# A two-layer Hawk and HGRN2 step: the fourth gate block in three passes, the gates by Silu, and a last stage in four spans

## The chip, the cores and the metric

The kernel runs on one core of a Trainium2 chip. Its time is the device time of one launch in microseconds (us). TensorE (PE in the profile, with PEld for its weight loads), VectorE (DVE), ScalarE (ACT), GpSimd (POOL) and SyncE (SP, which here only starts transfers) each run their own instruction stream and wait for one another by semaphores. Three runs of the kernel before gave 1030.36, 1031.57 and 1032.78 us, so the median is 1031.57 us.

## The reference

Two layers work on 1056 tokens: one prompt of 1024 and 8 short sequences of 4. Each layer normalises its input, multiplies it by one wide matrix, mixes along time, gates, multiplies by an output matrix and adds the input. Cut to what matters here:

```
u = rmsnorm(x) @ w_in;  xb, gate = u[:1536], u[1536:]
xc = causal_conv4(xb)
r  = sigmoid(xc_block @ w_r + b_r)      # 16 blocks of 96 channels
ig = sigmoid(xc_block @ w_i + b_i)
a  = exp(-8 * softplus(-lam) * r)
h  = scan(a, sqrt(1 - a*a) * (ig * xc))
x1 = x + (h * silu(gate)) @ w_out       # end of the first layer
q, f, v, g = split(rmsnorm(x1) @ b_w_in)
...                                     # HGRN2: chunked recurrence with a matrix state, 8 heads
x2 = x1 + (rmsnorm(o) * silu(g)) @ b_w_out
y  = rmsnorm(x2) * final_gain           # the last stage
```

The model is 1024 wide and the recurrence 1536. Everything is float32.

## The kernel before

**Layout.** Tokens lie along the free axis, channels along the partitions. In the first layer the 1056 columns are worked in three chunks of 352 (CH). The wide products are not made in plain float32: each operand is split into a high part in the float32r type and a remainder, also float32r, and mm3 (L262 to L264) adds three matmuls into one PSUM tile: high by high, high by low, low by high. So "a product over k" is three instructions, with two weight tiles. Weights come from HBM as float32 and are split by ACT (L403) and by POOL or DVE (L346).

**The first layer.** The 1536 channels are four groups (g) of 384, each in three tiles (j) of 128 partitions. For a group the program makes the product, the convolution (L521, L524), the split of the result into X (L529 for the high part), the gate products and the recurrence (lru). A gate block has 96 channels, a tile 128. So a group has four blocks on three tiles: three blocks lie whole on one tile each, the fourth has 32 rows on each of the three. The first three blocks take three passes each from X. For the fourth, three transfers per chunk collect the float32 rows into the tile ST (36 transfers in all), and one plain float32 matmul (L592) multiplies them with the weights gs; its result td goes by Tanh (L594) and three more transfers into R. The recurrence then uses Exp (L601, L603) and Sqrt (L611) on ACT. The output gate silu(z) is made from Tanh: ACT writes tanh(z/2) (L546, L553, L556), DVE adds 1 and multiplies by z (L557 and its two sisters), and a factor 0.5 goes into the product with h (L638).

**Order.** A class Flow holds every operation with its engine, a cost in us, what it reads and writes, and a priority; it plans all engines against each other, forward and backward, then searches, and emits each engine's list in the planned order. The wide products are main operations, whose order on PE is the program's; small products on PE (gates, norm sums, spreads) are not, and the planner puts them between main ones, held back by a slack `side` (1.2 us in the first layer). For ACT the planner charges 1.29 us when the function set changes and holds that Tanh, Exp and Silu are one set and Sqrt another.

**Norms.** The sum of squares over channels is a matmul of the squares with a column of ones (norm_sum, L299), which leaves one number per token on the partition axis. ACT takes the root, DVE the reciprocal. To spread the factor over the partitions, DVE multiplies it into the identity (a diagonal tile dg, L473 and L476 in the first layer, L1728 and L1732 at the end), and one float32 matmul of ones with dg (L478, L1738) gives the factor of each token on all partitions.

**Start.** While the first data arrives PE gets 36 float32 products of ones with ones (WARM, L753), lowest in priority, so that the planner may use them as filling.

**Last stage.** The output product of the second layer is made over column spans (OUT): 512, 288 and 256. In each span eight tiles (m) of 9 matmuls are added to x1 by DVE (L1781) and squared by ACT (L1783), and POOL adds up the squares (L1792). The sums of a span, as a main operation, come before product 3 of the next (RM), the spread before product 6 (SM); then finish multiplies eight tiles by the factor and by the gain: three with ACT (L1755) and POOL (L1756) after ACT has copied the factor out of PSUM (L1751), five on DVE (L1758), and sends each to HBM (L332), alternately from SP's and ACT's queue. In the last span the last squares go straight into the sum on PE, and two products (L1796) fill PE until the spread.

Of the kernel before, what the change touches and what calls it, by code (L numbers as in the profile page):

```python
# [14 lines left out]
F32 = mybir.dt.float32  # L15
# [4 lines left out]
ALU = mybir.AluOpType  # L20
PSUM = bass.MemoryType.PSUM
KB = 5
WARM = 36
# [11 lines left out]
RM, SM = 3, 6  # L35
OUT = ((0, 512), (512, 288), (800, 256))
# [194 lines left out]
def tile_trunk(ctx: ExitStack, tc: tile.TileContext, xT, prm, hc, w0, wg, wo0, w1, wo1, s_in,  # L231
# [41 lines left out]
    ones = const.tile([128, 128], F32, name="ones")  # L273
# [22 lines left out]
    def norm_sum(sums, acc, n, start, stop):  # L296

        for s, (a, u) in zip(sums, spans(n)):
            T.matmul(s[:u], acc[:, a:a + u], ones[:, :1], start=start, stop=stop)  # L299
# [18 lines left out]
    with ExitStack() as l0:  # L318
# [39 lines left out]
        gs = fixed("gs", [96, 2, 96])  # L358
# [10 lines left out]
        xos = ring("xo", NXO)  # L369
# [7 lines left out]
        ST = C("ST")  # L377
        rows = [C("sg") for _ in range(6)]
# [81 lines left out]
        def norm(acc, own=None, sums=None, sumk=()):  # L460
# [3 lines left out]
            dg, dk = own or next(xbs)  # L464
# [4 lines left out]
            for i, (s, (_, u)) in enumerate(zip(sums, spans(CH))):  # L469
# [17 lines left out]
        def conv(g, head=False):  # L487

            items = []
            for j in range(3):  # L490
# [3 lines left out]
                def evac(c, ps, pk, by=None, j=j, m=m, mine=mine):  # L494
# [31 lines left out]
                    w = slice(32 * j, 32 * j + 32)  # L526
                    dma(ST[w, chunk(c)], t[w], (tk,), (("ST", j, c),), 1, 45)
# [9 lines left out]
        def gate(g, js=range(3), late=False):  # L537

            items = []
            for j in js:  # L540

                def evac(c, ps, pk, by=None, j=j):
                    sg, sk = sgs[g][j, c] = halves[g % 2][3 * j + c]
                    if late:
                        t, tk = next(ts)
                        act(CH, lambda: S.activation(t, ps[:, :CH], AF.Tanh, scale=0.5), (pk,), (tk,), 0)  # L546
                        dve(CH, lambda: V.scalar_tensor_tensor(t, t, 1.0, ps[:, :CH], op0=ALU.add, op1=ALU.mult), (pk, tk), (tk,), 0)
                        dve(CH, lambda: V.scalar_tensor_tensor(sg, sg, 0.5, t, op0=ALU.mult, op1=ALU.mult), (tk, sk), (sk,), 1, True)
                        return
                    if by:  # L550
                        t, tk = next(ts)
                        dve(CH, lambda: V.tensor_tensor(sg, ps[:, :CH], by[0], op=ALU.mult), (pk, by[1]), (sk,), 0)
                        act(CH, lambda: S.activation(t, sg, AF.Tanh, scale=0.5), (sk,), (tk,), 0)  # L553
                        dve(CH, lambda: V.scalar_tensor_tensor(sg, t, 1.0, sg, op0=ALU.add, op1=ALU.mult), (tk, sk), (sk,), 1, True)
                        return
                    act(CH, lambda: S.activation(sg, ps[:, :CH], AF.Tanh, scale=0.5), (pk,), (sk,), 0)  # L556
                    dve(CH, lambda: V.scalar_tensor_tensor(sg, sg, 1.0, ps[:, :CH], op0=ALU.add, op1=ALU.mult), (pk, sk), (sk,), 0)  # L557
# [4 lines left out]
        def lru(g):  # L562
# [9 lines left out]
            dma(gs.rearrange("p a b -> p (a b)"), wg[g][:96, 768:], (), (("gs",),), 2, 74)  # L572
            prev = [(0.0, None)] * 3
            for c in range(NCH):
# [3 lines left out]
                ta, ti = R[:, 0], R[:, 1]  # L578
                tak, tik = ([("R", s, i, j) for j in range(3)] for i in range(2))
                for i, hb in ((0, hbr), (1, hbi)):  # L580
                    for j in range(3):
# [10 lines left out]
                    fl.add("PE", 0.62, lambda ps=ps, i=i, c=c: T.matmul(ps[:96, :CH], gs[:, i, :], ST[:96, chunk(c)], start=True, stop=True),  # L592
                           (("gs",), *(("ST", j, c) for j in range(3))), (pk,), 0)
# [21 lines left out]
                for j in range(3):  # L615
# [22 lines left out]
                    dve(CH, lambda h=h, sg=sg: V.scalar_tensor_tensor(sg, h, 0.5, sg, op0=ALU.mult, op1=ALU.mult), (hk, sk), (sk,), 3, True)  # L638
# [34 lines left out]
        def out_last(src):  # L673
# [42 lines left out]
            for c in range(NCH):  # L716
# [11 lines left out]
                for m, x, xk in rows:  # L728
                    scaled_parts(c, m, x, xk, bc, bk, pc("g1", m), ("P",), G if m % 4 == 3 else V, 4)
                    dma(xnd[m][:, chunk(c)], x, (xk,), (("xnd", m, c),), 5)  # L730

        def first1(i, c):
# [8 lines left out]
            else:  # L741
                t, tk = next(ts)
                act(CH, lambda: S.activation(t, ps[:, :CH], AF.Tanh, scale=0.5), (pk,), (tk,), 0)
                for o, a, b, ks in ((ST, lc, lbc, [("ST", j, c) for j in range(3)]), (a_rows[0], lcn, lc, [("a", 0, c)])):
# [5 lines left out]

        warm, wk = next(hg)
        for _ in range(WARM):
            fl.add("PE", 0.25, lambda: T.matmul(warm[:, :128], ones, ones, start=True, stop=True), (), (wk,), 9)  # L753
# [121 lines left out]
        rest += [(ST[:, :512], *(("ST", j, c) for j in range(3) for c in range(2)))]  # L875
        raw1 = [(), rest[:1], rest[1:3], rest[3:5], (), ()]

        def begin(c, first, last):
# [18 lines left out]
            bc, bk = norm(accs[c], next(xrs))  # L897
# [54 lines left out]
    with ExitStack() as l1:  # L952
# [760 lines left out]
        accs, sqs, dgs, sb = cycle(spare[:2]), cycle(spare[2:5]), cycle(spare[5:7]), spare[7]  # L1713
        nr2 = cycle([(fixed(f"nr2{i}", [128, 4], F32, p1), ("nr2", i)) for i in range(2)])

        def roots(n, sums, ready):

            r, rk = next(nr2)
            dg, dk = next(dgs)
            f, u = n // 128, n % 128  # L1720
# [7 lines left out]
            dve(128 * f, lambda: V.tensor_tensor(dg[:, :128 * f].rearrange("p (i n) -> p i n", i=f),  # L1728
                                                 ident[:, None, :].to_broadcast([128, f, 128]),
                                                 r[:, :f, None].to_broadcast([128, f, 128]), op=ALU.mult), (rk,), (dk,), 0)  # L1730
            if u:
# [138 lines left out]
```

## Time and profile before

| view | figure |
|---|---|
| profiled execution, its time | 1031.86 us |
| its span (first to last instruction) | 1030.1 us |
| median of three runs | 1031.57 us |
| PE busy | 1021.1 us, 99% |
| DVE busy | 810.8 us, 79% |
| ACT busy | 578.1 us, 56% |
| POOL busy | 496.5 us, 48% |
| ACT table loads | 34, mean 1.283 us |
| granted TensorE clock | 0.997 |
| start of the last stage's products | 981.12 us |
| last product pass issued, sums begin | 1019.1 to 1019.23 us |

A row of the timeline reads: start in us, duration in us, engine, line, operation, output<-input, size, and in brackets the idle time ahead of it with what ended that. Matmuls overlap in the array, so a matmul's duration is longer than the distance to the next one. What a matmul costs PE is the distance from start to start. Plain float32 matmuls leave two records each (the fourth block's row with "x2" is one instruction), float32r ones leave one.

### The profile page before, as it was taken

The page shows a single profiled execution, that of the slowest core. Times are in us where ns is not written, and L with a number is a line of the kernel's source. Part 1 is how long each engine was busy: PE and PEld are TensorE (multiplying, and loading weights), DVE is VectorE, ACT ScalarE, POOL GpSimd, SP SyncE. Part 2 cuts the span into 40 slices and gives each one's busy share as a digit, 9 for nine tenths or more (in the row PEclk, how much of TensorE's full clock was granted, in tenths as well). Part 3 has the DMA queues.
Part 4 walks back from the last instruction along what each step waited for, and adds up shares of the span by engine and source line. Part 5 has one row for each costly group of instructions (what it writes and reads, how often), then busy time and mean ns, then how long its engine had stood idle before and what let it go on. Part 6 is the DMA issues. An engine that isn't in the chain of part 4 may idle for free.

```text
span 1030.1 us, 26451 instructions
## 1 busy us (share of the span) xinstructions
PE 1021.1 (99%) x10118; PEld 996.4 (97%) x10118; DVE 810.8 (79%) x1641; ACT 578.1 (56%) x1322; POOL 496.5 (48%) x569
## 2 busy tenths in 40 slices
PE   9999999999999999999999999999999999999997
PEld 9999999999999999999999999999999999999986
DVE  7999785867888699436599999798989799986436
ACT  8788747876775785335454463626363636552334
POOL 0117353544526236636425656555555557533544
PEclk9999999999999999999999999999999999999998
DMA  9201112112852487426474244343535353687204
GB/s 299 78 17 56 57 48 74 52 54 76 257 178 59 133 270 223 160 83 219 136 213 138 73 147 132 130 148 111 167 111 168 102 159 122 207 246 209 87 1 169
DMA packets 107854, 138.30 MB, mean 134 GB/s; under 512 B 23632, under 2 KB 85072, under 8 KB 107728
## 3 DMA queue, kind: packets, MB, share of 16 engines
q1 hardware_dynamic: 105424, 133.85, 42.1%
q10 hardware_dynamic: 2304, 2.77, 0.8%
q8 instruction: 79, 1.29, 0.5%
q14 instruction: 47, 0.39, 0.1%
HBM read 89.99 MB, written 41.61 MB: 128 GB/s over the span
## 4 chain that ended last, share of the span: by engine, by line
PE 93%; DVE 2%; DMA 2%; ACT 1%; issue 1%; POOL 1%; SPq 0%; POOLq 0%; DVEq 0%; ACTq 0%
PE mm L262 27%; PE mm L264 26%; PE mm L263 26%; PE hg L1085 2%; PE hg L592 1%; PE hg L262 1%; PE hg L264 1%; PE hg L263 1%; PE hg L753 1%; PE hg L1232 1%; PE hg L1287 1%; PE hg L1289 1%; DMA k<-yd 1%; PE mm L1085 0%; DMA vt<-sg 0%
## 5 line engine op out<-in xcount | busy, mean ns | idle before, releaser
L262 PE MATMUL mm<-xh,whi 128*128 128x352 f32 (+1 forms) x1127 | 352.6, 313 | 0.1
L264 PE MATMUL mm<-xh,wlo 128*128 128x352 f32 (+1 forms) x1127 | 348.1, 309 | 0.0
L263 PE MATMUL mm<-xl,whi 128*128 128x352 f32 (+1 forms) x1127 | 347.7, 309 | 0.0
L346 POOL TENSOR_TENSOR wlo<-wraw,whi 128x256 fp32r<-128x256 f32 (+3 forms) x188 | 200.8, 1084 | 199.7 <-ACT whi L403 97.3
L263 PEld LDWEIGHTS mm<-xl,whi 128*128 128x128 f32 x1127 | 212.5, 189 | 1.4 <-DVE xl L346 0.3
L262 PEld LDWEIGHTS mm<-xh,whi 128*128 128x128 f32 x1127 | 211.8, 188 | 2.1 <-DVE k L1545 0.3
L264 PEld LDWEIGHTS mm<-xh,wlo 128*128 128x128 f32 x1127 | 212.0, 188 | 0.0
L524 DVE SCALAR_TENSOR_TENSOR k<-xb,prm_sb,k 128x352 f32<-128x352 f32 (+2 forms) x144 | 82.3, 596 | 24.2 <-ACT k L521 20.7
L262 PE MATMUL mm<-t,whi 128*128 128x264 f32 (+1 forms) x330 | 96.6, 293 | 0.2 <-issue 0.2
L264 PE MATMUL mm<-t,wlo 128*128 128x264 f32 (+1 forms) x330 | 94.4, 286 | 0.0
L263 PE MATMUL mm<-t,whi 128*128 128x264 f32 (+1 forms) x330 | 94.4, 286 | 0.0
L1545 DVE TENSOR_TENSOR k<-mm,k 128x264 f32<-128x264 f32 x154 | 64.0, 424 | 11.7 <-PE mm L264 10.3
L346 POOL TENSOR_TENSOR wlo<-R,whi 128x256 fp32r<-128x256 f32 x70 | 58.3, 854 | 27.0 <-ACT whi L1469 24.1
L607 POOL TENSOR_TENSOR k<-X 128x352 f32<-128x352 f32 x36 | 43.6, 1217 | 52.8 <-DVE R L608 42.0
L1469 ACT CAST whi<-wraw 128x512 fp32r<-128x512 f32 x56 | 34.5, 618 | 60.4 <-DVE wraw L1479 26.0
L403 ACT CAST whi<-wraw 128x512 fp32r<-128x512 f32 (+2 forms) x79 | 44.3, 572 | 39.1 <-PE mm L263 28.9
L262 PEld LDWEIGHTS mm<-t,whi 128*128 128x128 f32 x330 | 62.1, 188 | 1.5 <-issue 0.3
L263 PEld LDWEIGHTS mm<-t,whi 128*128 128x128 f32 x330 | 62.2, 188 | 0.0
L264 PEld LDWEIGHTS mm<-t,wlo 128*128 128x128 f32 x330 | 62.1, 188 | 0.0
L262 PE MATMUL mm<-yh,whi 128*128 128x352 f32 x153 | 52.2, 341 | 0.0
L264 PE MATMUL mm<-yh,wlo 128*128 128x352 f32 x153 | 49.4, 323 | 0.0
L263 PE MATMUL mm<-yl,whi 128*128 128x352 f32 x153 | 49.4, 323 | 0.0
(458 smaller groups left out, 2513.9 us busy)
## 6 DMA issues: line engine op xcount, KB each, us to landing
wraw<-in_w_dram SPq DMA_DIRECT2D x88, 256.0 KB, 3.0
wraw<-in_wo_dram SPq DMA_DIRECT2D x34, 192.0 KB, 2.5
R<-in_w_dram SPq DMA_DIRECT2D x17, 256.0 KB, 3.9
si<-in_s_in_dram SPq DMA_DIRECT2D x8, 512.0 KB, 5.4
vt<-sg SPq DMA_DIRECT2D x8, 512.0 KB, 3.8
sg<-vt SPq DMA_DIRECT2D x32, 128.0 KB, 2.9
kt<-kt SPq DMA_DIRECT2D x8, 512.0 KB, 3.6
kt<-kt SPq DMA_DIRECT2D x32, 128.0 KB, 5.1
```

The costliest lines, as they stand in the source:

```text
L262: T.matmul(out, wh, xh, start=first, stop=False)
L263: T.matmul(out, wh, xl, start=False, stop=False)
L264: T.matmul(out, wl, xh, start=False, stop=last)
L346: emit = lambda: e.tensor_tensor(b, x, a.bitcast(F32), op=ALU.subtract)
L403: act(m, lambda hi=hi, raw=raw, m=m: S.copy(hi[:, :m], raw[:, :m]), rk, (hk,), prio)
L524: dve(u, lambda src=src, dst=dst, sh=sh, k=k: V.scalar_tensor_tensor(dst, sh(src, k), pc("cw", 12 * k + m), dst, op0=ALU.mult, op1=ALU.add ...
L592: fl.add("PE", 0.62, lambda ps=ps, i=i, c=c: T.matmul(ps[:96, :CH], gs[:, i, :], ST[:96, chunk(c)], start=True, stop=True), (("gs",), *((" ...
L607: pool(CH, lambda x=x, a=a, b=b: G.tensor_tensor(x, a.bitcast(F32), b.bitcast(F32), op=ALU.add), (ak, bk), (xk,), 3)
L753: fl.add("PE", 0.25, lambda: T.matmul(warm[:, :128], ones, ones, start=True, stop=True), (), (wk,), 9)
L1085: T.matmul(ps[32 * j:32 * j + 32, n * w:n * w + w], B[:, o:o + 32], q(slice(o, o + 32)), start=True, stop=True, tile_position=(0, 32 * j))
L1469: act(512, lambda: S.copy(hi, raw), (rk,), (hk,), 2)
L1545: dve(QT, lambda: V.tensor_tensor(o[0], z[0], u[0], op=ALU.add), (z[1], u[1]), (o[1],), 0)
```

## The change

- **Fourth gate block.** No rows go into ST any more. For each chunk the 32 rows of each tile's high and low part are gathered from X into a tile G4 with a ring of three slots, so six transfers where there were three (72 in all). The weights are loaded raw and split into gsh and gsl, and the block is one mm3 of three float32r passes. ST is used for the squares of the first norm instead.
- **Filling.** WARM goes from 36 to 26, and the products are made from another tile filled with ones; `ones` shrinks to one column.
- **Spread.** spread_rows makes, for each 128 columns, one float32 matmul whose weights are the factor's column broadcast to 128, and whose moving tile is the identity. DVE's diagonal tiles are gone, in the first layer and at the end.
- **Gates.** Each of the first layer's 36 gates is one Silu on ACT. The DVE operation after it is gone, and the factor 0.5 with it.
- **Last stage.** Spans 448, 288, 192 and 128. Sums and spread of a span are no longer main operations; they are added ahead of the next span's first product and the planner places them, with a slack of 0.1 us. Squares of the tiles 6 and 7 are added on DVE instead of POOL. A transfer's size is given to the planner as 0.37n instead of n/2.

```diff
-WARM = 36
+WARM = 26
-OUT = ((0, 512), (512, 288), (800, 256))
+OUT = ((0, 448), (448, 288), (736, 192), (928, 128))
...
+    def spread_rows(bc, r, n):
+        for i, (a, u) in enumerate(spans(n)):
+            T.matmul(bc[:, a:a + u], r[:u, i:i + 1].to_broadcast([u, 128]), ident[:u, :u], start=True, stop=True)
...
-            dve(256, lambda: V.tensor_tensor(dg[:, :256].rearrange("p (i n) -> p i n", i=2),
-                                             ident[:, None, :].to_broadcast([128, 2, 128]),
-                                             r[:, :2, None].to_broadcast([128, 2, 128]), op=ALU.mult), (rk,), (dk,), 0)
-            dve(96, lambda: V.tensor_scalar(dg[:, 256:CH], ident[:, :96], r[:, 2:3], None, op0=ALU.mult), (rk,), (dk,), 0)
-            fl.add("PE", 0.7, lambda: T.matmul(bc[:, :CH], ones, dg[:, :CH], start=True, stop=True), (dk,), (bk,), 0)
+            fl.add("PE", 0.7, lambda: spread_rows(bc, r, CH), (rk,), (bk,), 0)
...
-                    dma(ST[w, chunk(c)], t[w], (tk,), (("ST", j, c),), 1, 45)
...
-                    act(CH, lambda: S.activation(sg, ps[:, :CH], AF.Tanh, scale=0.5), (pk,), (sk,), 0)
-                    dve(CH, lambda: V.scalar_tensor_tensor(sg, sg, 1.0, ps[:, :CH], op0=ALU.add, op1=ALU.mult), (pk, sk), (sk,), 0)
+                    act(CH, lambda: S.activation(sg, ps[:, :CH], AF.Silu), (pk,), (sk,), 0)
...
-            dma(gs.rearrange("p a b -> p (a b)"), wg[g][:96, 768:], (), (("gs",),), 2, 74)
+            dma(raw[:96, :192], wg[g][:96, 768:], (), (rk,), 2, 74)
+            act(192, lambda raw=raw, hi=hi: S.copy(hi, raw[:96, :192]), (rk,), (("gsh",),), 2)
+            pool(192, lambda raw=raw, hi=hi, lo=lo: G.tensor_tensor(lo, raw[:96, :192], hi.bitcast(F32), op=ALU.subtract),
+                 (rk, ("gsh",)), (("gsl",),), 2)
...
+                own = [next(sts) for _ in range(2)]
+                both = [G4[:, q] for q in own]
+                for j in range(3):
+                    for i, o in enumerate(both):
+                        x, xk = xpart(j, i, c)
+                        dma(o[w].bitcast(F32), x[w].bitcast(F32), (xk,), (("g4", j, own[i]),), 1, 45)
...
-                    fl.add("PE", 0.62, lambda ps=ps, i=i, c=c: T.matmul(ps[:96, :CH], gs[:, i, :], ST[:96, chunk(c)], start=True, stop=True),
+                    fl.add("PE", 0.48, lambda ps=ps, i=i, both=both: mm3(ps[:96, :CH], (gsh[:, i], gsl[:, i]), *both, True, True),
...
-            fl.add("PE", 0.002 * n, lambda: T.matmul(bc[:, :n], ones, dg, start=True, stop=True), (dk,), (bk,), 0, main=main)
+            fl.add("PE", 0.0023 * n, lambda: spread_rows(bc, r, n), (rk,), (bk,), 0, main=main)
...
-            fl.add("PE", 0.7, lambda: norm_sum(sums, acc, n, True, True), (ak,), (sk,), 0, main=True)
+            fl.add("PE", 0.7, lambda: norm_sum(sums, acc, n, True, True), (ak,), (sk,), 0)
...
-                if a and m == RM:
-                    dg = summed(*prev[:2], prev[3])
-                if a and m == SM:
-                    finish(*prev[2:], *spread(prev[3], *dg, True))
+                if a and m == 0:
+                    scales = summed(*prev[:2], prev[3])
+                    finish(*prev[2:], *spread(prev[3], *scales, False))
...
+                elif m > 5:
+                    dve(n, lambda acc=acc, sq=sq, n=n: V.tensor_tensor(acc[:, :n], acc[:, :n], sq[:, :n], op=ALU.add), (sk, ak), (ak,), 1, True)
```

The planner places everything in the first layer anew. The second layer's list on PE, up to the last stage, is the same in both. Three places matter below.

PE at the start of the program, before (xh and xl are the parts of the first layer's input, whi and wlo the weight parts; four of the 36 fillers between the third and the fourth product):

```order
L262 MATMUL mm<-xh,whi 128x352
L263 MATMUL mm<-xl,whi 128x352
L264 MATMUL mm<-xh,wlo 128x352
L753 MATMUL hg<-ones 128x128 x4
L262 MATMUL mm<-xh,whi 128x352
L263 MATMUL mm<-xl,whi 128x352
```

And after, from the first row of PE's list:

```order
L763 MATMUL hg<-cst 128x128 x26
L261 MATMUL mm<-xh,whi 128x352
L262 MATMUL mm<-xl,whi 128x352
L263 MATMUL mm<-xh,wlo 128x352
L261 MATMUL mm<-xh,whi 128x352
```

In both, 26 fillers stand ahead of the first product. The ten others of before, such as the four in the first piece, are gone, and the first products follow one another without any.

ACT in the first layer, before, at a first gate (L556) between a weight cast (L403), the gate blocks' Tanh (L588, L594) and the recurrence's Exp (L601); the row ACT_TABLE_LOAD is the load of a function table:

```order
L556 ACT_TABLE_LOAD
L556 ACTIVATE sg<-mm 128x352
L403 CAST whi<-wraw 128x512
L508 COPY xb_137<-mm 128x320
L588 ACTIVATE R<-hg,smalls 128x352
L594 ACTIVATE td<-hg,smalls 96x352
L516 COPY xb_137<-mm 128x8x4
L521 ACTIVATE k<-xb_137,prm_sb 128x320
L403 CAST whi<-wraw 128x512
L601 ACTIVATE a<-R,smalls 128x352
```

ACT after, where the gate is L553, the blocks' Tanh L596 and L602, the cast L410 and the Exp L609 and L611:

```order
L596 ACTIVATE R<-hg,smalls 128x352
L410 CAST whi<-wraw 128x512
L602 ACTIVATE td<-hg,smalls 96x352
L553 ACTIVATE sg<-mm 128x352
L410 CAST whi<-wraw 128x512
L609 ACT_TABLE_LOAD
L609 ACTIVATE a<-R,smalls 128x352
L611 ACTIVATE R<-R,smalls 128x352
```

Between the gate's function and the Exp a table is now loaded, where before none stood. In the whole list of ACT the table loads go from 34 to 51.

PE at the end, before: the last product of the 256 span, the sums (L299), the two fillers and the spread:

```order
L264 MATMUL mm<-t_5211,xl 128x256
L299 MATMUL hg<-ones,R 128x1 x2
L299 MATMUL hg<-ones,sg 128x1 x2
L299 MATMUL hg<-ones,a 128x1 x4
L299 MATMUL hg<-ones,sg 128x1 x2
L1796 MATMUL mm<-ones 128x128 x2
L1738 MATMUL hg<-sg,ones 128x256
```

And after, where L303 is spread_rows, first for the 192 span and, behind the last product of the 128 span, for that span itself:

```order
L263 MATMUL mm<-t_5257,xl 128x128
L303 MATMUL mm<-ident,nr_5276 128x128
L303 MATMUL mm<-ident,nr_5276 128x64
L261 MATMUL mm<-t_5254,xl 128x128
...
L298 MATMUL hg<-ones,R 128x1
L298 MATMUL hg<-ones,a 128x1 x2
L298 MATMUL hg<-ones,sg 128x1
L298 MATMUL hg<-ones,a 128x1
L1801 MATMUL mm<-ident 128x128 x2
L303 MATMUL hg<-ident,nr_5277 128x128
```

The spread of the 192 span stands ahead of the last product of the 128 span, and that of the last span is one matmul of 128 columns.

More of the change, by code (lines that the diff above doesn't have):

```diff
@@ L272, in tile_trunk @@
     make_identity(nc, ident)
-    ones = const.tile([128, 128], F32, name="ones")
+    ones = const.tile([128, 1], F32, name="ones")
     V.memset(ones, 1.0)
@@ L298, in norm_sum @@
         for s, (a, u) in zip(sums, spans(n)):
-            T.matmul(s[:u], acc[:, a:a + u], ones[:, :1], start=start, stop=stop)
+            T.matmul(s[:u], acc[:, a:a + u], ones, start=start, stop=stop)
+    def spread_rows(bc, r, n):
+        for i, (a, u) in enumerate(spans(n)):
+            T.matmul(bc[:, a:a + u], r[:u, i:i + 1].to_broadcast([u, 128]), ident[:u, :u], start=True, stop=True)
     def new_acts():
@@ L377, in tile_trunk @@
         ST = C("ST")
+        xos = cycle([(ST[:, chunk(i)], ("ST", i)) for i in range(NXO)])
+        G4 = fixed("G4", [96, NCH, CH], F32R)
+        sts = cycle(range(NCH))
         rows = [C("sg") for _ in range(6)]
@@ L458, in squares, with norm @@
                 (pool if e is G else dve)(CH, lambda: e.tensor_tensor(a[:, :CH], a[:, :CH], sq, op=ALU.add), (sk, ak), (ak,), 2)
-        def norm(acc, own=None, sums=None, sumk=()):
+        def norm(acc, sums=None, sumk=()):
             a, ak = acc
             r, rk = next(nrs)
-            dg, dk = own or next(xbs)
             if sums is None:
@@ L748, in tile_trunk @@
         ws1 = {}
+        fill = cst.rearrange("p m b j -> p (m b j)")[:, :128]
+        V.memset(fill, 1.0)
         warm, wk = next(hg)
         for _ in range(WARM):
-            fl.add("PE", 0.25, lambda: T.matmul(warm[:, :128], ones, ones, start=True, stop=True), (), (wk,), 9)
+            fl.add("PE", 0.25, lambda: T.matmul(warm[:, :128], fill, fill, start=True, stop=True), (), (wk,), 9)
         g0 = fixed("g0", [128, 8])
@@ L896, in begin @@
                 dma(hct, hc, (), (("hct",),), 2, 196)
[L897 removed]
+            bc, bk = norm(accs[c])
             if c == 0:
@@ L1795, in tile_trunk @@
         for _ in range(2):
-            fl.add("PE", 0.45, lambda: T.matmul(spin[:, :128], ones, ones, start=True, stop=True), sumk, (wk,), 0)
+            fl.add("PE", 0.45, lambda: T.matmul(spin[:, :128], ident, ident, start=True, stop=True), sumk, (wk,), 0)
         finish(a, n, *spread(n, *roots(n, sums, sumk), False))
```

44 lines of the change are left out of this document (18 added, 26 removed).

## The prediction

> **What bounds the kernel now.** I read the page first: its busy shares, the granted clock in 40 slices and the shares of the chain of waits.
>
> ```profile
> span 1030.1 us, 26451 instructions
> PE 1021.1 (99%) x10118; PEld 996.4 (97%) x10118; DVE 810.8 (79%) x1641; ACT 578.1 (56%) x1322; POOL 496.5 (48%) x569
> PEclk9999999999999999999999999999999999999998
> PE 93%; DVE 2%; DMA 2%; ACT 1%; issue 1%; POOL 1%; SPq 0%; POOLq 0%; DVEq 0%; ACTq 0%
> ```
>
> PE is busy in 99% of the span, at full clock to the last slice. Next I read what PE waits for (output, line, the releaser, then us, times, longest).
>
> ```profile
> PE hg L753 <- DVE nr L365: 1.0, 1, 1.0
> PE hg L1738 <- DVE sg L1728: 0.7, 2, 0.5
> ```
>
> One wait ahead of the first filler, and two at the last stage's spreads. In the first layer, once it runs, PE never waits. So a term counts in full if it shortens or lengthens PE's own stream, or lies behind its last product; work taken from DVE or ACT counts only where PE would otherwise wait.
>
> **The fourth gate block.** The timeline of PE at one block of before; the row of two records is the float32 matmul.
>
> ```profile
> 62.10 0.33 PE L264 MATMUL mm<-xh,yl 128*128 128x352 f32 x1
> 62.26 0.76 PE L592 MATMUL hg<-ST,gs 96*96 96x352 f32 x2
> 62.59 0.59 PE L262 MATMUL mm<-xh,yh 128*128 128x352 f32 x1
> 63.02 0.32 PE L263 MATMUL mm<-xl,yh 128*128 128x352 f32 x1
> ```
>
> A float32r pass of 352 columns takes 62.26 − 62.10 = 0.16 us. From 62.26 to 63.02 there is one float32 matmul and one pass, so the matmul costs 0.76 − 0.16 = 0.60. Three passes cost 0.48. With 4 groups, 3 chunks and 2 gates that is 24 × −0.11 = **−2.6 us**, certain as long as the parts are there in time. Its price is transfers on SP's queue, 72 where there were 36. One row of the tile ST's transfers:
>
> ```profile
> L332 SPq DMA_DIRECT2D ST<-k x36: 507/512/592, 41.5 to 354.1; - x36
> ```
>
> The queue's time of one is 0.51 us, so 36 more are 18.4 us in some 310, 6%. Each starts after ACT's high part or DVE's low part, not after the convolution, so a block's data comes about two operations later (0.5 us each, next part). The planner places the block with that knowledge, and other products cover it: zero, with rival 3 if not.
>
> **Fillers.**
>
> ```profile
> 10.84 0.32 PE L264 MATMUL mm<-xh,wlo 128*128 128x352 f32 x1
> 11.00 1.05 PE L753 MATMUL hg<-ones 128*128 128x128 f32 x8
> 11.81 0.41 PE L262 MATMUL mm<-xh,whi 128*128 128x352 f32 x1
> 12.05 0.33 PE L263 MATMUL mm<-xl,whi 128*128 128x352 f32 x1
> 12.37 0.69 DVE L346 TENSOR_TENSOR wlo<-a,whi 128x512 fp32r<-128x512 f32 x1 [0.25 <-ACT whi L403]
> ```
>
> From 11.00 to 12.05 PE issues four fillers (eight records) and a pass: 1.05 − 0.16 = 0.89, or 0.22 each. The first 26 stay ahead of the data; the ten others stand between products, so dropping them saves up to **−2.2 us**. The other end is 0: the weight part at 12.37 is ready at 13.06, and if such data sets the pace, PE waits where it filled. I take −2.2, since PE had no wait there and DVE's early list gets shorter too.
>
> **First-layer spread.** Twelve spreads: one float32 matmul of 352 columns (0.60) becomes three of 128, 128 and 96. By the filler, 128 cost 0.22, so three cost about 0.65: 12 × 0.05 = **+0.6 us** at most. DVE's diagonals go, off PE's path.
>
> **Last stage on PE.** The starts of the spans' products and sums in the timeline:
>
> ```profile
> 981.12 0.39 PE L262 MATMUL mm<-t,xh 128*128 128x512 f32 x1
> 997.78 0.29 PE L262 MATMUL mm<-t,xh 128*128 128x288 f32 x1
> 1001.41 0.95 PE L299 MATMUL mm<-ones,R 128*128 128x1 f32 x8
> 1002.22 0.38 PE L262 MATMUL mm<-t,xh 128*128 128x288 f32 x1
> 1009.59 0.28 PE L262 MATMUL mm<-t,xh 128*128 128x256 f32 x1
> 1012.77 0.65 PE L299 MATMUL hg<-ones,R 128*128 128x1 f32 x6
> ```
>
> Each span has 8 × 9 = 72 matmuls. 512 columns: 16.66/72 = 0.231. 288: three products of 9 in 3.63, 0.134. 256: 3.18/27 = 0.118. The line through these has 0.00046 per column, so 448 cost 0.203. By it 192 would cost 0.089 and 128 0.061. But every matmul of a product has a new weight tile, and what a load costs by itself is seen where one column moves, PEld at the first sums:
>
> ```profile
> 1001.27 1.00 PEld L299 LDWEIGHTS mm<-ones,R 128*128 128x128 f32 x8
> 1002.19 0.19 PEld L262 LDWEIGHTS mm<-t,xh 128*128 128x128 f32 x1
> ```
>
> Eight loads in 0.92, 0.115 each, with nothing to stream behind them. The 256 span at 0.118 lies on that floor. I take 0.113 for the two narrow spans, a little under it: 72 × (0.203 + 0.134 + 2 × 0.113) = 40.5 against 72 × (0.231 + 0.134 + 0.118) = 34.8, **+5.7 us**. Bounds: −5.4 + 5.7 = about +0.5 if narrow matmuls follow the line (rival 2), +29 if they fall to the float32 rate (rival 4). A third set of sums and spreads adds ten one-column matmuls' worth and some float32 passes, about 1.1; the two waits ahead of spreads, now placed by the planner, give back 0.4 of 0.7: **+0.7 us**.
>
> The Trainium skill, in "TensorE: Matmul & The Clock Gate", section "LDWEIGHTS (loading the stationary operand)", gives columns divided by 1.2 ns, or 107 ns for 128, which the trace's 0.115 roughly bears out; by that figure the narrow spans would cost 0.9 us less. The same page's "Back-to-back issue gap" has pairs of load and matmul sustained at about 81 ns for 128 columns; no run here shows that, and by it the 128 span alone would be 2.3 us shorter, a step towards rival 2.
>
> **The tail.** From the first sums behind the last span's products to the end:
>
> ```profile
> 1019.23 0.50 PE L299 MATMUL hg<-ones,R 128*128 128x1 f32 x4
> 1019.92 0.51 DVE L1758 SCALAR_TENSOR_TENSOR a<-a,prm_sb,mm 128x288 f32<-128x288 f32 x1
> 1020.34 0.42 DVE L1781 TENSOR_TENSOR sg<-mm,sg 128x256 f32<-128x256 f32 x1
> 1020.86 0.42 ACT L1783 ACTIVATE sg<-sg 128x256 f32<-128x256 f32 x1 [0.18 <-DVE sg L1781]
> 1021.33 0.61 PE L299 MATMUL hg<-ones,sg 128*128 128x1 f32 x4 [0.26 <-ACT sg L1783]
> 1021.75 0.48 ACT L1724 ACTIVATE nr<-hg,eps 128x1 f32<-128x1 f32 x2
> 1022.46 0.42 DVE L1728 TENSOR_TENSOR sg<-ident,nr 128x256 f32<-128x256 f32 x1
> 1022.94 0.70 PE L1738 MATMUL hg<-sg,ones 128*128 128x256 f32 x2 [0.46 <-DVE sg L1728]
> 1023.68 0.37 ACT L1751 COPY sg<-hg 128x256 f32<-128x256 f32 x1 [1.45 <-PE hg L1738]
> 1024.13 2.09 POOL L1756 TENSOR_TENSOR sg<-sg 128x256 f32<-128x256 f32 x3 [3.45 <-ACT sg L1751]
> 1026.43 0.42 ACTq L332 DMA_DIRECT2D out_yT_dram<-sg  x1
> ```
>
> It takes 1030.1 − 1019.23 = 10.87 us. The last add (1020.34) stood behind finish's multiplications; those of the 192 span are shorter, −0.4. The add and the square each halve in columns, −0.2. One root instead of two, −0.2. No diagonal: 1022.46 to 1022.94, −0.48. The spread falls from 256 float32 columns to 128, −0.2, the copy −0.1. POOL's three multiplications take 0.70 each; at half the columns I take 0.42 (between proportional 0.35 and no change), −0.85. DVE's five shrink alongside. The closing transfer carries half the bytes, −0.2 at most. I take **−2.7 us**; bounds −1.8 (POOL alone shrinks little) and −3.2.
>
> **The gates.** From the groups of DVE and ACT, and the busy time of PE, PEld, DVE, ACT and POOL, then clock, DMA share and GB/s, in one stretch of the first layer:
>
> ```profile
> L557 DVE SCALAR_TENSOR_TENSOR sg<-sg,mm 128x352 f32<-128x352 f32 x27 | 13.9, 513 | 6.1 <-ACT sg L556 5.9
> L611 ACT ACT_TABLE_LOAD x12 | 15.4, 1283 | 0.2
> L556 ACT ACT_TABLE_LOAD x7 | 9.0, 1283 | 0.1
> L594 ACT ACT_TABLE_LOAD x5 | 6.4, 1283 | 0.1
> 50.00:100.00 50.00, 50.00 (x304) 48.82 (x303) 47.88 (x123) 42.57 (x86) 21.97 (x29) 1.00 0.13 38
> ```
>
> DVE loses 36 operations of 0.51, 18.5 us; it is busy 47.9 us of these 50, so that is room, though PE did not wait for it. ACT gains 17 table loads of 1.283, 21.8 us, which the planner does not know, since it holds Silu and Exp to be one set. On average that is 6% of the layer's some 355 us; in the stretch above ACT would go from 42.6 to about 49 of 50 at five loads per 50 us. Bounds: 0, if PSUM tiles and operands are always ready earlier than needed, as before, when the 24 loads of these groups left PE no wait; 21.8, if each load delays PE in full. I take **+1.0 us**, near the lower end: one or two chunks where a Tanh behind a load frees a PSUM tile late. Without DVE's spare time to absorb it, that would be rival 1.
>
> The Trainium skill, in "ScalarE: Activation LUTs", section "Table sets: the hidden batching unit", has one set active at a time and about 2.7 us per load; the trace's 1.283 decides, and by 2.7 the 17 loads would be 46 us of ACT.
>
> **Sum.** −2.6 − 2.2 + 0.6 + 5.7 + 0.7 − 2.7 + 1.0 = +0.5, some of it upper ends, so +0.3. The profiled execution before took 1031.86 us for its span of 1030.1, 0.3 above the median 1031.57 and within the runs' spread of 1030.4 to 1032.8. From the median that makes **1031.9 us**: no change that can be measured. What can't be told from no change is 0.2%, or 2.1 us: 1029.5 to 1033.6.
>
> **Rivals.**
>
> 1. *ACT falls behind.* The loads stand between the gate's Silu and the recurrence's Exp, and behind them the Tanh that frees the next gate product's PSUM tile. For: ACT's 42.6 of 50, and a planner that plans without them. Against: no PE wait at those 24 loads before. It decides from two to three loads' worth of PE waits on. With four: 1031.9 − 1.0 + 5.1 = 1036.0, slower.
> 2. *Narrow spans follow the line.* Then the two cost 72 × (0.089 + 0.061) = 10.8 instead of 16.3, −5.4, and DVE (a narrow add, a multiplication and a late square per tile) gives back about 1.9: 1028.4, faster. For: the line is straight from 512 to 256. Against: PEld's 0.115.
> 3. *The gathers come late.* Waits at the fourth block, 24 places; with 0.2 us each, 1031.9 + 5 = 1037. For: twice the transfers. Against: 6% of a queue.
> 4. *Narrow float32r matmuls run at the float32 rate* (0.60/352 per column): 0.327 and 0.218, 72 × 0.545 = 39.2 against 16.3, +23: about 1055. For: the trace has no float32r product under 256 columns that could exclude it. Against: the line shows no step down to 256.
>
> **Chances.** The forecast has 0.58: of it 0.40 within the bound, 0.10 faster (no PE wait from ACT, tail at −3.2, floor lower: 1029.5), 0.08 slower (fillers worth nothing: 1034.1). Rival 1 has 0.17, of it 0.15 slower and 0.02 within; rival 2 0.14, faster; rival 3 0.04 and rival 4 0.07, slower. Together: faster 0.24, same 0.42, slower 0.34. The forecast's own range is 1029.5 to 1034. To leave out no more than 2 in 10 the range goes to 1027.5, past rival 2, and to 1037, past rival 1 with four loads, and leaves out rival 4, half of rival 3 and the tails of 1 and 2.
>
> **What would show it.** Right: passes of the fourth block 0.16 apart; products at the start without fillers and without PE waits; the 192 and 128 spans both near 0.113 per matmul, so about 8.1 us each without sums; a tail near 8.2 us; 51 table loads and under 2 us of PE waits on ACT in the first layer. Wrong: PE waits of more than 3 us there (rival 1), a 128 span of under 6 us (rival 2) or over 14 (rival 4), waits for G4 (rival 3), or a wait at the start near 13 us that eats the fillers' gain.

## The result, and the profile after

The changed kernel takes 1042.41 us (median of 4 runs, 1040.05 to 1043.54), the kernel before 1032.17 us beside it: a ratio of 1.0102, 95% interval 1.0083 to 1.012. It is 10 us slower; the forecast was no change, 1031.9 us, and the range ended at 1037.

Two things said ahead of the prediction have to be put right. Of the recurrence's two functions on ACT, L601 (L609 after) is an Exp, L603 (L611) a Tanh. And the list of the change leaves out one edit: in the last chunk of the first layer's output, two of the eight low parts are subtracted on DVE instead of POOL. No run tells that one apart.

The page of the changed kernel: span, busy times, shares of the chain of waits.

```profile
span 1040.3 us, 26742 instructions
PE 1027.0 (99%) x10226; PEld 1008.7 (97%) x10226; DVE 786.9 (76%) x1613; ACT 604.7 (58%) x1356; POOL 494.8 (48%) x575
PE 83%; ACT 7%; DVE 4%; DMA 3%; issue 1%; SPq 1%; POOL 0%; ACTq 0%; DVEq 0%
```

ACT has gained 26.6 us, DVE lost 23.9. The chain that ended last ran through PE for 93% before and for 83% now; 7% of it is ACT. Where that comes from is seen in the waits of PE between 20 and 565 us, a stretch in which the kernel before has none (output, line, the releaser, then us, times, longest):

```profile
PE mm L261 <- ACT sg L553: 1.8, 1, 1.8
PE mm L261 <- DVE sg L550: 1.2, 1, 1.2
PE hg L261 <- ACT R L596: 1.0, 1, 1.0
PE hg L261 <- ACT td L602: 0.6, 1, 0.6
PE hg L262 <- DVE X L530: 0.6, 1, 0.6
PE mm L261 <- ACT xh L486: 0.5, 1, 0.5
PE hg L261 <- ACT X L529: 0.3, 1, 0.3
```

The second layer's first product, the first of 264 columns, marks the end of the first layer: 566.84 us, 6.25 later than before (560.59). The second layer up to the last stage takes 420.3, as before (420.5). The rest is the last stage. Its spans' starts, and then its end, in the timeline:

```profile
987.13 0.37 PE L261 MATMUL mm<-t,xh 128*128 128x448 f32 x1
...
1001.72 0.29 PE L261 MATMUL mm<-t,xh 128*128 128x288 f32 x1
...
1013.46 0.25 PE L261 MATMUL mm<-t,xh 128*128 128x192 f32 x1
...
1022.08 0.33 PE L261 MATMUL mm<-t,xh 128*128 128x128 f32 x1
...
1032.11 0.27 PE L261 MATMUL mm<-t,xl 128*128 128x128 f32 x1
...
1032.22 0.28 PE L262 MATMUL mm<-t,xl 128*128 128x128 f32 x1
1032.33 0.28 PE L263 MATMUL mm<-t,xl 128*128 128x128 f32 x1
...
1032.45 0.33 PE L298 MATMUL hg<-ones,R 128*128 128x1 f32 x2
...
1034.29 0.26 ACT L1732 ACTIVATE nr<-hg,eps 128x1 f32<-128x1 f32 x1 [0.48 <-POOL sg L1759]
...
1034.80 0.49 PE L303 MATMUL hg<-ident,nr 128*128 128x128 f32 x2 [0.44 <-DVE nr L1735]
...
1035.67 1.28 POOL L1759 TENSOR_TENSOR sg<-sg 128x128 f32<-128x128 f32 x3 [1.57 <-ACT sg L1754]
...
1037.71 0.41 ACTq L336 DMA_DIRECT2D out_yT_dram<-sg  x1
```

The 192 span takes 8.62 us with one set of sums in it, the 128 span 10.37 with one set of sums and the spreads of the 288 and 192 spans: the narrower one is not faster, and its last matmuls stand 0.11 us apart. Products and sums together take 1032.45 − 987.13 = 45.3 us where they took 1019.23 − 981.12 = 38.1. The tail takes 1040.3 − 1032.45 = 7.85 where it took 10.87: the last stage is 4.2 us slower.

How a wait of the first layer comes about, at the longest, 227 us. ACT's and PE's rows of the timeline:

```profile
222.12 1.28 ACT L619 ACT_TABLE_LOAD   x1
...
224.86 1.28 ACT L596 ACT_TABLE_LOAD   x1
...
226.16 0.56 ACT L596 ACTIVATE R<-hg,smalls 128x352 f32<-128x352 f32 x1
...
227.03 0.32 PE L263 MATMUL mm<-xh,wlo 128*128 128x352 f32 x1
...
227.33 1.28 ACT L553 ACT_TABLE_LOAD   x1
228.63 0.46 ACT L553 ACTIVATE sg<-mm 128x352 f32<-128x352 f32 x1
...
229.15 0.43 PE L261 MATMUL mm<-xh,whi 128*128 128x352 f32 x1 [1.79 <-ACT sg L553]
...
230.28 0.49 PE L261 MATMUL mm<-xh,whi 128*128 128x352 f32 x1
230.57 0.49 PE L262 MATMUL mm<-xl,whi 128*128 128x352 f32 x1
...
233.51 0.35 PE L263 MATMUL mm<-xh,wlo 128*128 128x352 f32 x1
```

Three loads in 6.5 us: for the root (L619), for the Tanh behind it (L596), and for the Silu. The third is there only because the gate is a Silu, and it stands ahead of the operation that empties the PSUM tile that PE needs next. Behind the wait comes something unforeseen: from 230.28 to 233.51 eleven passes are 0.293 apart instead of 0.161, 1.46 us lost. The slices of the page's clock row, 26 us each, are too long to show it. Asked for this stretch alone, the trace has PE's granted clock at 0.50 (the stretch, its length, PE's busy time and instructions, granted clock, DMA share, GB/s):

```profile
230.13:233.53 3.40, 3.40 (x14) 0.50 0.21 62
```

Not all of the waits have a load right ahead of them. Those at 195 us (on L602) and 229 us (on L553) do, 2.4 of the 6.0 us. Before the one at 388 us (on L596) ACT itself had sat idle for 2.5 us until a weight's transfer landed, and the one near 27 us (on L550) is on DVE.

### The profile page after: what moved, and what is told of

The parts are those of the page before. It is cut to its first block, busy times and chain, and to the rows that moved or that the text cites. A ratio compares the mean times of both kernels' runs of the same rounds, so it can differ in the third digit from the quotient of the medians.

```text
span 1040.3 us, 26742 instructions
## 1 busy us (share of the span) xinstructions
PE 1027.0 (99%) x10226; PEld 1008.7 (97%) x10226; DVE 786.9 (76%) x1613; ACT 604.7 (58%) x1356; POOL 494.8 (48%) x575
## 4 chain that ended last, share of the span: by engine, by line
PE 83%; ACT 7%; DVE 4%; DMA 3%; issue 1%; SPq 1%; POOL 0%; ACTq 0%; DVEq 0%
PE mm L261 24%; PE mm L263 23%; PE mm L262 23%; PE hg L1095 2%; PE hg L262 1%; PE hg L261 1%; PE hg L263 1%; PE hg L1242 1%; PE hg L1297 1%; ACT a L609 1%; DMA k<-yd 1%; PE hg L1299 1%; ACT R L611 1%; SPq L336 1%; DMA wraw<-in_w_dram 1%
## 5 line engine op out<-in xcount | busy, mean ns | idle before, releaser
L410 ACT CAST whi<-wraw 128x512 fp32r<-128x512 f32 (+2 forms) x79 | 44.1, 571 | 36.3 <-PE mm L262 21.0
L261 PE MATMUL mm<-yh,whi 128*128 128x352 f32 x153 | 49.5, 324 | 0.0
```

The costliest lines, as they stand in the source:

```text
L261: T.matmul(out, wh, xh, start=first, stop=False)
L410: act(m, lambda hi=hi, raw=raw, m=m: S.copy(hi[:, :m], raw[:, :m]), rk, (hk,), prio)
```

## The experiments

Fourteen kernels, each timed beside the kernel before (1032.0 to 1032.6 in these comparisons). The first two keep every list's order, so that no new plan is mixed in. Single traces scatter too: in five kernels with the same list up to there, PE's first product starts at 8.35 to 9.83 us.

**Tanh for Silu in the changed kernel.**

```diff
-                    act(CH, lambda: S.activation(sg, ps[:, :CH], AF.Silu), (pk,), (sk,), 0)
+                    act(CH, lambda: S.activation(sg, ps[:, :CH], AF.Tanh), (pk,), (sk,), 0)
...
```

> The changed kernel with the gates' Silu replaced by Tanh of the same size and nothing else: the gates' values are left wrong, every list keeps its order, and ACT has 34 table loads instead of 51. Theory A (the table loads delay the ACT operations that free PSUM tiles, and PE waits): the PE waits of the first layer, about 9 us with the refill behind them, and the half-clock stretch near 230 us, 1.5 us, go, and the time falls from 1042.4 to 1032 to 1034. Theory B (the new order, the missing fillers and the gathers make the waits, the loads lie beside other work): 1041 to 1042.5. If only the waits directly behind a load go, about 4 us: 1037 to 1039.

Measured: 1034.7 us, ratio 1.0025 (1.001 to 1.004) against 1.0102, just above theory A's 1032 to 1034. Taking the loads away gives back 0.77%, 7.7 us by the medians. It is the loads and not the function: an operation of L553 takes 0.465 us with Silu and with Tanh. In the trace the first layer ends at 557.81, 9.0 earlier, and of PE's waits between 20 and 557 us one is left; the second layer takes 1.8 us longer here (422.05 against 420.29). The wait that is left, and L553's loads, in the changed kernel and here:

```profile
PE mm L261 <- DVE sg L550: 0.6, 1, 0.6
```

```profile
L553 ACT ACT_TABLE_LOAD x10 | 12.8, 1283 | 1.4 <-PE mm L263 1.3
L553 ACT ACT_TABLE_LOAD x3 | 3.8, 1283 | 0.1
```

The waits on L486, L529 and L530 go with those on Silu and Tanh, though these are not the operations that a load stands ahead of: a load makes ACT late for what is queued behind it. The wait on L550 is another matter. It stands near 27 us, ahead of the first load that Silu adds (33.7 us), so that it shrinks here isn't the loads' doing.

**Silu for Tanh in the kernel before.**

```diff
-                    act(CH, lambda: S.activation(sg, ps[:, :CH], AF.Tanh, scale=0.5), (pk,), (sk,), 0)
+                    act(CH, lambda: S.activation(sg, ps[:, :CH], AF.Silu, scale=0.5), (pk,), (sk,), 0)
...
```

> The kernel before with the gates' Tanh replaced by Silu in place (the operations behind it kept, so the gates' values are wrong), every list in the order of before, 50 table loads instead of 34. Theory A: PE waits of 5 to 10 us appear in the first layer, 1037 to 1042. Theory B: no change, 1031.5 to 1033.

Measured: 1038.01 us, ratio 1.0058 (1.0045 to 1.0071), so 5.4 us. PE's waits between 20 and 567 us, where the kernel before has none:

```profile
PE hg L262 <- ACT R L588: 1.0, 2, 0.8
PE mm L262 <- DVE sg L552: 0.9, 1, 0.9
PE mm L263 <- DVE xl L346: 0.8, 2, 0.5
PE hg L592 <- ACT td L594: 0.4, 1, 0.4
PE mm L262 <- ACT xh L484: 0.3, 1, 0.3
PE hg L263 <- DVE X L530: 0.3, 1, 0.3
```

The same cause acts in the old order too; theory B falls as an explanation of most of the loss.

**The old spans.**

```diff
-OUT = ((0, 448), (448, 288), (736, 192), (928, 128))
+OUT = ((0, 512), (512, 288), (800, 256))
```

> The changed kernel with the last stage's spans of before (512, 288, 256), all else as changed; the first layer is the same list. By the traces the last stage on PE grew by 7.2 us and the tail shrank by 3.0, so this gives 4.2 us back: 1038 (1036.5 to 1039.5). If the cost of the narrow spans were hidden: 1042.

Measured: 1038.73 us, ratio 1.0056 (1.0041 to 1.0071): 3.7 us back, as the traces had it.

**The gates of before, planned anew.**

```diff
-                    act(CH, lambda: S.activation(sg, ps[:, :CH], AF.Silu), (pk,), (sk,), 0)
+                    act(CH, lambda: S.activation(sg, ps[:, :CH], AF.Tanh, scale=0.5), (pk,), (sk,), 0)
+                    dve(CH, lambda: V.scalar_tensor_tensor(sg, sg, 1.0, ps[:, :CH], op0=ALU.add, op1=ALU.mult), (pk, sk), (sk,), 0)
...
```

> The changed kernel with the gates of before (Tanh, then the DVE operations, the factor 0.5), planned anew. Theory A: the first layer loses its waits on ACT and keeps the fourth block's -2.7 and the fillers' gain of up to 3.1; with the last stage's +4.2 and perhaps 1.5 us of waits at the start that is 1030 to 1033. Theory B: 1040 to 1043.

Measured: 1042.3 us, ratio 1.0097 (1.0082 to 1.0111), nothing gained with 17 loads fewer: a miss for theory A alone. PE's waits between 20 and 565 us:

```profile
PE mm L261 <- DVE sg L552: 1.6, 1, 1.6
PE hg L261 <- ACT R L600: 1.1, 1, 1.1
PE hg L262 <- DMA G<-X: 0.4, 1, 0.4
PE mm L262 <- DVE xl L350: 0.4, 1, 0.4
...
```

Now DVE, which has its gate operations back, is late, ACT once (at 387 us), and once the gathers. So the loads are not the only thing that can use up the cover. That led to theory C (it is the order of any new plan) and the next four runs.

**The fourth block alone, in the kernel before.** The edit is the change's own part, with the ones as a broadcast column for want of space.

> The kernel before with the fourth gate block of the change alone (three passes on gathered parts; the squares of the first norm in ST; the ones as a broadcast column, for space). Gates by Tanh, 36 fillers, spans of before. Theory A (the loads for Silu make the waits): the block's 2.7 us are gained in full, 1029 to 1030.5. Theory C (every new plan of the first layer brings waits that the planner's costs do not foresee, the loads only being the largest of them): PE waits of 2 to 6 us in the first layer eat the gain, 1031 to 1036. If the gathers themselves come late, the waits name G4.

Measured: 1036.11 us, ratio 1.0037 (1.0023 to 1.0051). But it isn't a clean trial: the diagonal tile of the spread and a first weight share a space here, and most of its waits, 6.0 us by the starts of the passes, lie before 45 us.

**26 fillers alone, in the kernel before.**

```diff
-WARM = 36
+WARM = 26
```

> The kernel before with 26 fillers instead of 36 and nothing else, planned anew. If the ten dropped fillers had covered nothing: 1029.5 to 1030.5 (2.2 us less). If they stood where the data of the first 30 us is late anyway: waits of 1 to 2 us near 26 us, 1031.5 to 1033. Theory C: further waits elsewhere in the first layer, 1032 to 1036.

Measured: 1032.3 us, ratio 1.0001 (0.9991 to 1.0011). The ten fillers cost nothing that can be measured; the first layer ends at 560.32, 0.3 earlier, and a wait of 0.4 on a DVE gate has come in near 27 us.

**Another seed.**

```diff
-rng = Random(1)
+rng = Random(2)
```

> The changed kernel with the gates of before, as the run with Tanh gates planned anew, and the planner's search started from another seed, so that only the order in the first layer differs. Theory C: another time by 2 to 8 us either way (1034 to 1044), with other waits. If the waits came from the parts of the change rather than from the order: within 1.5 us of 1042.

Measured: 1042.71 us, ratio 1.0101 (1.0082 to 1.012). Another order in hundreds of rows, the same time, and the waits at the same places (near 28, 41, 277 and 385 us). As far as one other seed tells, chance in the search is not the cause; theory C in that form falls.

**A planner that knows the loads.**

```diff
-    SETS = {"Sqrt": 1, "Tanh": 2, "Exp": 2, "Silu": 2}
+    SETS = {"Sqrt": (1,), "Tanh": (2, 3), "Exp": (2,), "Silu": (3,)}
...
```

> The changed kernel with Silu, and a planner that holds Exp and Silu for two sets, Tanh for a member of both, and charges 1.29 us for each change; 58 table loads stand in its list, seven more than unknown ones before. If a load that the planner knows of is placed where it harms nothing: PE waits in the first layer under 4 us, 1034 to 1037. If the number of loads decides: 1042 to 1046.

Measured: 1039.36 us, ratio 1.0069 (1.005 to 1.0088), between the two expectations, with 58 loads instead of 51. So more loads need not cost more: where they stand counts. In its trace no PE wait on ACT is left, but two on the gathers, 2.0 us together, and some on DVE, 1.6 us.

That made theory D: the fourth block's data now comes after the split and six transfers, a chunk's chain is longer, and what ACT or DVE has on top becomes a wait.

**Block and spread, then with 26 fillers, in the kernel before.** The change's parts, gates and last stage of before; the second run has WARM = 26.

> The kernel before with the fourth gate block and the first layer's spread of the change, and nothing else of it: gates by Tanh, 36 fillers, last stage of before. Against the run with the block alone the diagonal tiles are gone, for which a first weight had taken the space and made a wait of 1.3 us at 35 us. If the new plan of the first layer can hide the gathers: 1030 (-2.7 + 0.5). Theory D (the fourth block's data now comes after the split and six transfers, so a chunk's chain is longer, and with DVE's gate operations of before DVE is late too, and PE waits): waits of 3 to 6 us, 1033 to 1036.

> As the run with block and spread, with 26 fillers. By the run with 26 fillers alone the ten dropped ones gain nothing: within 1.5 us of the run with block and spread. If they gain where all 36 stand ahead of the first product: 1 to 2 us less.

Measured: 1035.57 us, ratio 1.0036 (1.0023 to 1.0049), and 1042.48 us, ratio 1.0101 (1.0084 to 1.0118). The first is theory D's 3 to 6 us less the stream's gain. The second is a surprise: ten fillers less cost 7 us here and nothing in the kernel before. PE's waits with 26 fillers, between 5 and 567 us and then between 568 and 980 us:

```profile
PE mm L262 <- ACT xh L488: 1.8, 1, 1.8
PE mm L262 <- DVE sg L554: 1.5, 1, 1.5
PE mm L263 <- POOL xl L352: 1.3, 1, 1.3
...
```

```profile
PE mm L262 <- DVE k L1559: 1.0, 1, 1.0
PE mm L1246 <- issue: 0.6, 1, 0.6
PE mm L263 <- POOL xl L352: 0.6, 1, 0.6
...
```

With 36 fillers the wait of the first row, near 38 us, is not there, and that of the second, near 27 us, is down to 0.5. The 36 delay the first product by 2.3 us (11.71 against 9.40), so, as I read it, PE starts later and does not overtake ACT and DVE. With a stretch of slow passes behind them the two make some 4 us, but the products also start earlier, and the first layer ends only 2.8 us later (567.77 against 564.93). The other 4.1 us by the traces lie in the second layer (423.15 against 419.09), though its list on PE is the same; what makes DVE and POOL late there isn't explained.

**Without the gathers, order kept**, first with the gates of before, then in the changed kernel.

```diff
-                both = [G4[:, q] for q in own]
+                both = [xpart(0, q, c)[0][:96] for q in range(2)]
...
-                        dma(o[w].bitcast(F32), x[w].bitcast(F32), (xk,), (("g4", j, own[i]),), 1, 45)
+                        fl.add("SP", 0.45, lambda: None, (xk,), (("g4", j, own[i]),), 1, 45.0)
```

> The run with Tanh gates planned anew, every list in its order, without the 72 gathers: the fourth block reads 96 rows of one tile's parts in X instead (so its gates' values are wrong). Theory D: the waits at 276 and 382 to 385 us, about 2.2 us, go, and those near 27 and 40 us with the half-clock stretch behind them, about 4 us, stay if they have to do with the norm and not with the block: 1039 to 1041. If the gathers bear on all of it: 1035 to 1037. If on nothing: 1042.

> The changed kernel in its order, with Silu and 51 table loads, without the 72 gathers in the same way. Theory A alone (the loads make the waits): 1041 to 1043. Theory D: the loads' waits are there because the gathers have already used up the slack; 1 to 4 us less, 1038 to 1041.

Measured: 1039.64 us against 1042.3, ratio 1.0076 (1.0059 to 1.0092), and 1039.11 against 1042.4, ratio 1.0065 (1.0051 to 1.0078). 2.7 and 3.3 us, about as much as the three passes save; the first of the two is not clear of noise, since the intervals overlap (1.0082 to 1.0111 with the gathers). The waits at 276 and 382 to 385 us go in the one, those at 195 and 387 us in the other, while most of the early ones stay: theory D. The one near 27 us is gone in the changed kernel without gathers, but the first gather starts at 45 us; PE's first product started 1.1 us later in this trace (9.83 against 8.74). PE's longest waits that are left there:

```profile
PE mm L261 <- ACT sg L553: 1.7, 1, 1.7
PE hg L262 <- DVE X L530: 0.9, 2, 0.6
...
```

**All three undone** (Tanh for Silu, no gathers, the old spans), each as above, first layer in the change's order.

> The changed kernel's first layer in its order with Tanh of the same size in place of Silu (34 table loads) and without the 72 gathers (both leave the gates' values wrong), and the spans of before in the last stage. If the three costs of the single runs add up (7.7, 3.3 and 3.7 us): 1042.4 - 14.7 = 1027.7, which would leave the stream's gains of the prediction, some 4 us under the kernel before. If loads and gathers bear on the same waits: 1030 to 1031.

Measured: 1029.71 us, ratio 0.9973 (0.9963 to 0.9984): 12.7 us less than the changed kernel, 2.0 short of the sum of the single effects, which is no more than the intervals leave open. But the traces say the same: without the loads the first layer ends at 557.69 without gathers and at 557.81 with them, so there the gathers cost nothing. By the times they cost 1034.7 − 1029.7 − 3.7 = 1.3 us at most. So loads and gathers bear in part on the same waits. What is left of the change is worth 2.8 us against the kernel before.

**36 fillers in the changed kernel.**

> The changed kernel with 36 fillers, planned anew; 49 table loads. If the dropped fillers had covered the waits near 26 and 41 us, as the runs with the fourth block and 26 against 36 fillers have it: 1036 to 1040. If the fillers do nothing beside the loads and the gathers: 1041 to 1044.

Measured: 1040.19 us, ratio 1.0083 (1.0067 to 1.0099), 2.2 us less than with 26, at the edge of what was expected and not clear of noise (1.0083 to 1.012 with 26). In the trace the waits near 26, 41 and 75 us are gone. Here dropping ten fillers saved nothing, and by the medians it cost what it was to save.

No kernel that computes the reference beat the kernel before by more than the comparisons can tell. The one run below it has gates with neither DVE's operation nor a table load, and no gathers; a version that has this and computes the gates was not found.

## Why the prediction was wrong, step by step

- **What bounds the kernel.** Right as read: PE's stream, full, with no wait. Wrong was what I made of it, that each part may be costed alone as long as the engine beside PE has time on average. The cover is one and the same for loads, gathers and DVE's operations, and the kernel before had hardly any to spare: 16 loads more in its own order cost it 5.4 us.
- **The gates, +1.0.** This is the step that failed most: 7.7 us. I had the 17 loads, their 1.283 us and the bounds of 0 and 21.8, and chose near the lower one because 24 loads had left PE without a wait. But those were known to the planner and stood where it had left room for 1.29 us; the new ones were not. The row that should have decided, as I now see it, was ACT's 42.6 busy us of 50. The mechanism is rival 1's, though only 2.4 of the 6.0 us of waits stand where it had them, at tiles freed by Silu and Tanh right behind a load; all the others but the one on L550 go when the loads go, and a stretch at half the clock adds 1.46. Rival 1's price of 5.1 was too small as well.
- **Fourth block, −2.6.** PE's part was right. One block in the timeline after; the last row is the next block's:

```profile
195.61 0.40 PE L261 MATMUL hg<-G,gsh 96*96 96x352 f32 x1 [0.60 <-ACT td L602]
195.85 0.32 PE L262 MATMUL hg<-G,gsh 96*96 96x352 f32 x1
196.01 0.32 PE L263 MATMUL hg<-G,gsl 96*96 96x352 f32 x1
196.17 0.32 PE L261 MATMUL hg<-X,gh 128*128 128x352 f32 x1
```

  Passes are 0.16 apart, and 0.24 here after a wait. But "other products cover it: zero" failed for the gathers: 2.7 to 3.3 us beside late engines, by the traces nothing where ACT is on time. That is rival 3, which I gave 0.04; I weighed the queue's load (6%) instead of the length of the chain.
- **Fillers, −2.2.** Measured −0.2 in the kernel before and +2.2 in the changed one, neither clear of noise. My other end, 0, was the better one. I had named the weight part that was barely in time, and set it aside for DVE's shorter list; the waits came later, near 26 and 41 us, on gates and parts of the norm.
- **First-layer spread, +0.6.** No run tells it apart. There are 6 spreads there, not 12 (12 was the number of records), so by its own reckoning the term is +0.3.
- **Last stage, +6.4, and tail, −2.7.** Measured +7.2 and −3.0 in the trace, +3.7 together in the runs against +3.7 forecast, an agreement that is partly luck, since both terms were too small in size. The narrow spans cost 0.112 a matmul, at 192 columns as at 128: the floor of the weight loads was right, rivals 2 and 4 were wrong. The excess of 0.8 lies in sums and spreads between the products. (The sum for rival 2's bound was misadded: −5.4 + 5.7 is +0.3, not +0.5. And the three wider spans' line has 0.00044 per column, which the 0.203 for 448 goes by, not 0.00046.)

The Trainium skill, in "TensorE: Matmul & The Clock Gate", section "LDWEIGHTS (loading the stationary operand)", divides the columns by 1.2, which for 128 gives an estimate of 107 ns for such a load; the trace has 112 from matmul to matmul at both widths. That page's 81 ns for pairs at 128 columns (section "Back-to-back issue gap") does not hold for these float32r products.

So the sum by effects, from the runs: −2.8 for what is left of the change against the kernel before, +3.7 for the spans, +1.3 at most for the gathers by themselves, +7.7 for the loads on top, together +9.9 of the measured 10.2. Each of these runs differs from the next by one part, so that the sum closes proves nothing; what shows the cause are the two runs in which the function alone was exchanged. What stays open is why a new plan with DVE's gate operations, which needs no more loads than before, isn't faster, beyond that its waits are on DVE, on gathers and once on ACT, and the unexplained part of the 7 us that ten fillers make with block and spread, most of it in the second layer.

## What to carry to other kernels

An operation moved from one engine to another is not free because that engine is 60% busy: look for what the planner does not know of it (here table loads, because Silu and Exp never ran under the same table, so that 34 became 51), and try it in the unchanged order first, with the function alone exchanged. Costs hidden by the same slack are not to be summed one by one: with the loads gone the gathers cost nearly nothing, with them 3 us. A narrower last tile shortens the tail, but its matmuls do not get cheaper without end: at 192 and at 128 columns one cost the same 0.112 us here, against 0.118 at 256. Where between 256 and 192 the floor begins wasn't tried.

## What was not expected of the hardware

A wait of PE can cost more than its length. In the traces of these kernels there are ten waits in the first layer of 1.65 to 2.24 us by the starts of the passes; behind six of them, 0.3 to 1.0 us after PE had gone on, the granted clock fell to 0.50 for 3.41 us, and 9 to 11 passes came at 0.293 instead of 0.161 us, about 1.2 to 1.5 us lost each time. Behind the other four, and behind all shorter waits, none came. It may be part of why executions of one kernel differ: of the twelve with Tanh for Silu, the nine with a mean clock of 0.997 or 0.998 took 1032.5 to 1036.5 us and the three with 0.993 took 1037.2 to 1041.2; where in those three the clock was low wasn't recorded.

The Trainium skill, in "TensorE: Matmul & The Clock Gate", warns in "HAM oscillation — how this bites in real kernels" of idle gaps over some 3.4 us; here waits of half that were enough, and the measurement decides. That the same wait does it in one kernel and not in another would fit the free-running window that the page describes; no run here tested it.
